# A fourth pair by seven products in the first gate block, two more in the second down block, and three groups of stored sums formed by adding transfers

## The chip, the cores and the metric

One NeuronCore of one Trainium2 chip. The metric is the device time of one execution in microseconds; lower is better. The kernel before was timed in three runs: 1460.48 us in the median (1459.78 to 1462.02).

## The reference, cut to what matters

A block of a hybrid model on 256 rows of 2048 columns, float32 throughout. The change touches the gates and the last product:

```python
proj = h @ w_in                     # h: 256 x 2048; the last 3 * 2048 columns are the gates
...
g = sigmoid(gates.reshape(b, s, 3, 2048) + b_gate)
merged = g[:, :, 0] * (o_fox @ w_br_fox) + g[:, :, 1] * (o_sb @ w_br_sb) + g[:, :, 2] * (o_mem @ w_br_mem)
x = x + merged @ w_out
u = conv(rms_norm(x) @ w_up)        # 2 * 5632 columns
x = x + (silu(u_gate) * u_val) @ w_down     # 256 x 5632 by 5632 x 2048: "down"
```

## The kernel before

**Three passes.** Every large product runs in fp32r: ACT makes a rounded copy `hi` of each weight tile (128 rows by 1024 columns, 512 KB) and DVE the remainder `lo` (`parts`, L349 to L356). Each 128x512 piece of a product is then three matmuls (`three`, L358 to L362): the high part of the activations with `hi`, their low part with `hi`, their high part with `lo`. There are four `hi` and four `lo` buffers.

**Blocks.** A gate, `w_out` or down product is done in blocks of 1024 output columns (`blocked`, L410). A block walks over pairs of 128-row weight tiles (2p and 2p + 1); a *plan*, a string such as `esesesee`, says how each pair is done, in order. `e` (`eight`) is the plain way: two weight tiles, eight 128x512 products, 24 matmuls. `s` is a Strassen-Winograd form with seven products, 21 matmuls. It needs four sums of quarters of the two weight tiles (T1 = B00 + B01, T3 = B01 + B11, T2 = T1 + B11, T4 = T2 + B10) and four sums of the activations' quarters. It has its own four PSUM banks `Y`, which are added into the result (`gathered`) after the block's last seven.

**Where the weights' sums come from.** In the gates `seven_here` is used: DVE forms the four sums from the two loaded tiles (`prepared`, L469 to L476, four additions of 512 columns), one pair ahead. In `w_out` and down `seven` is used (L444): the sums were formed earlier and stored to DRAM, and the pair loads 1.75 MB (two loads of 256 KB, one of 512 KB of the plain weights or sums, then 512 KB and 256 KB of sums) where `e` loads 1 MB. The deque `halves` lists what is to be stored; the helpers `first_sums`, `pair_sums_ahead` and `half_sums` load the plain weights on SP's queue, add on DVE (L252 to L256) and store. 35 pairs are stored, 10 for `w_out` and 25 for down.

**The activations' sums.** For the gates they are formed once for the first `GS = 3` pairs (`x_sums`, in the tile `xs`). For down they are formed by the plan's letter `f` (`form`, then `pair_sums` L365 to L378), 11 in the first down block and 3 in the second. Those of the second block are written over quarters of the activations `aT` that only its first eights still read.

**Order around the change.** The stages follow each other on TensorE: the first gate block done plainly (309.9 to 361.2 us), two gate blocks by plan, the branches, three gate blocks, the branches, `w_out`, up, and from 1232.2 us the two down blocks. In the gates and branches `keep_in_program_order` pins the matmuls; elsewhere the scheduler of the tile framework puts instructions on each engine's queue, and every queue runs in order. SP's queue issues nearly all loads; a load waits until DVE has read the buffer's last tenant (four such buffers in the gates, six in down). POOL's queue is idle between 338 and 760 us; at 760.2 us it moves the row scales of the hidden state.

Of the kernel before, what the change touches and what calls it, by code (L numbers as in the profile page):

```python
# [34 lines left out]
WBUFS = 4  # L35
SBUFS = 4
BLOCKS = 14
GS = 3
PF = (6, 5)
DU = 22  # L40

# [2 lines left out]
def hybrid_block(  # L44
# [159 lines left out]
    def k_tiles(name):  # L204
# [20 lines left out]


    o_plans = ("eessssse", "eessssse")
    g_plans = (("", "esesesee", "esesesee"), ("esesesee", "esesesee", "esesesee"))
    d_plans = (
        "efefefef" + "sef" * 4 + "ssefsfssfssee",  # L230
        "efefef" + "sss" + "esss" * 3 + "ssee",
    )
    T1, T3, T4, T2 = range(4)
    FS2, FS4, FS3, FS1 = range(4)
    in_order = tc.keep_in_program_order
    dram = ctx.enter_context(tc.tile_pool(name="dram", bufs=1, space=bass.MemoryType.DRAM))
    by_k = lambda w: w[0].rearrange("(k p) n -> p k n", p=P)
    o_sevens = (0, 1, 2, 3, 6)
    pairs = lambda name, n: o_sevens if name == "o" else range(n)
    sums_of = {}  # L240
    ordered = [False]
    halves = deque(
        (name, by_k(w), nb, pr, h)
        for name, w, plans in (("o", w_out, o_plans), ("d", w_down, d_plans))
        for nb, plan in enumerate(plans)
        for pr in pairs(name, plan.count("s"))
        for h in range(2)
    )

# [35 lines left out]
    def pair_sums_ahead(staging, period, add, store, most=99, delay=0):  # L285
# [31 lines left out]
        while due:  # L317
            step()
            clock += 1
            yield  # L320

    def first_sums():

# [75 lines left out]
    def blocked(name, w, nb, n0, plan, pair, sums, raw_tile, t4_tile, gathered, ready=None, form=None, apart=None):  # L399
# [1 line left out]
        wv = by_k(w)  # L401
        X = [[bank(f"x{name}{nb}_{t}_{n}") for n in range(2)] for t in range(NT)]
        Y = []
        ns = plan.count("s")

        def a_of(p, j, t):
            v = pair(p, j)
# [34 lines left out]
                                three(apart[0], *a_of(p, j, t), wj, j == 0, j == 1)  # L442

        def seven(p, first, last):  # L444
            kept = sums_of[name, nb, p]
# [6 lines left out]
            raw3 = t4_tile(f"raw_t4_{name}{nb}_{p}")  # L452
# [12 lines left out]
            three(X[1][0], *a_of(p, 1, 1), T4w)  # L465
            go_on()
# [27 lines left out]
        by_seven = seven_here if name == "g" else seven  # L494
        ahead = {}
        s, e = 0, 0
        sp = pairs(name, ns)
        ep = [p for p in range(len(plan) - plan.count("f")) if p not in sp]
        for i, c in enumerate(plan):
            if c == "s":  # L500
                if s == 0:
                    if ready:
                        ready()
                    Y += [bank(f"y{name}{nb}_{j}") for j in range(4)]
                by_seven(sp[s], s == 0, s == ns - 1)
                s += 1
                if s == ns:
                    later(gathered(n0, Y))
# [210 lines left out]
    w = {}  # L719
# [348 lines left out]
    for m in range(2):  # L1068
        gate = []
        for b, plan in enumerate(g_plans[m]):  # L1070
# [52 lines left out]
            for n in range(2):  # L1123
                scaled_sums(n, [X[t][n] for t in range(NT)], [g[n][:, t] for t in range(NT)])
                nc.scalar.activation(g[n], g[n], AF.Sigmoid)
        if m == 1:
            later(merged_sums())
        for n in range(2):
# [190 lines left out]
    def s_of(p, f):  # L1319
# [7 lines left out]
            return sf_more[0][:, f] if f < 2 else sf_rest[2]  # L1327
        if p == 10:
            return sf[:, 27] if f == 0 else sf_rest[f - 1]
        return a_blocks[:, 2 * (p - N0 + N1) + f // 2, :, f % 2]  # L1330

    tmp_d = lambda name: place([P, PIECE], F32, "ts", name)

# [66 lines left out]
```

## Time and profile before

| | |
|---|---|
| median of three runs | 1460.48 us |
| the profiled execution's own time | 1460.56 us |
| its span in the profile | 1458.8 us |
| granted TensorE clock | 1.00 in every slice |
| matmuls by lines L360 to L362 in a run without waits | one every 0.227 us |
| second and third gate block, start to start | 41.5 us, 41.6 us |
| second down block to the end of the span | 112.8 us |
| POOL busy | 21.4 us |

In the rows, PE is TensorE, PEld its weight loads, DVE VectorE, ACT ScalarE, POOL GpSimd and SP the queue that issues loads. A row of a timeline has the start, the duration, the engine, the line and the tiles; in brackets stands idle time before it and what ended it. Matmuls overlap, so that each lasts 0.39 us while the next starts 0.227 us after it. A tile `raw_...` is loaded from DRAM, `hi_...` and `lo_...` are its two parts, `t_...` holds sums, `kept_...` is a pair's sums in DRAM.

### The profile page before, as it was taken

To read this page: it belongs to the slowest core of one execution; us is meant where nothing else is said; L and a number is where in the kernel's file an instruction comes from. 1 tells how busy PE (TensorE), PEld (TensorE's weight loads), DVE (VectorE), ACT (ScalarE), POOL (GpSimd) and SP (SyncE) were. 2 spreads that over 40 slices of the span, in tenths; PEclk is the share of its full clock that TensorE was granted. 3 is DMA by queue.
4 is the path that set the end of the run, shared out by engine and by line. 5 is a ranking of instruction groups with operands and counts; after the bars stand their busy time and mean duration, and the time that the engine had idled before them with its cause. 6 is when DMAs were issued, how large, how long until landed. Compare 5 with 4: busy or idle time off the path is not lost.

```text
span 1458.8 us, 20569 instructions
## 1 busy us (share of the span) xinstructions
PE 1452.1 (100%) x7295; PEld 1228.4 (84%) x7295; DVE 1221.8 (84%) x1804; ACT 851.9 (58%) x1210; POOL 21.4 (1%) x52
## 2 busy tenths in 40 slices
PE   9999999999999999999999999999999999999998
PEld 7888878888888888888888888888888888888887
DVE  5788778776898899998987888888888877999878
ACT  6755445464564555546766656556556565676665
POOL 0000010010000000000000000000000000000000
PEclk9999999999999999999999999999999999999999
DMA  8797899777668576788877888888888866789896
GB/s 290 228 352 247 320 323 333 266 250 217 212 206 268 176 226 201 271 266 261 304 213 231 290 275 299 282 270 299 286 278 298 272 197 201 253 283 341 293 334 220
DMA packets 166502, 387.64 MB, mean 266 GB/s; under 512 B 12554, under 2 KB 29854, under 8 KB 162174
## 3 DMA queue, kind: packets, MB, share of 16 engines
q1 hardware_dynamic: 164702, 383.29, 79.2%
q10 hardware_dynamic: 1328, 2.11, 0.4%
q8 instruction: 57, 0.93, 0.3%
q0 software_dynamic: 368, 0.93, 0.2%
q14 instruction: 47, 0.39, 0.1%
HBM read 347.47 MB, written 38.80 MB: 265 GB/s over the span
## 4 chain that ended last, share of the span: by engine, by line
PE 95%; issue 1%; DVE 1%; DMA 1%; SPq 0%; ACT 0%; POOL 0%; DVEq 0%; POOLq 0%; ACTq 0%
PE u L1289 22%; PE u L1290 11%; PE xg L362 4%; PE xg L361 4%; PE xg L360 4%; PE xd L360 4%; PE xd L362 3%; PE xd L361 3%; PE s L362 2%; PE f L360 2%; PE s L360 2%; PE f L362 2%; PE f L361 2%; PE b L362 2%; PE s L361 2%; PE b L361 2%
## 5 line engine op out<-in xcount | busy, mean ns | idle before, releaser
L1289 PE MATMUL u<-hT,hi_u 128*128 128x512 f32 x1232 | 428.5, 394 | 0.0
L1290 PE MATMUL u<-hT,lo_u 128*128 128x256 f32 x1232 | 341.5, 277 | 0.0
L1289 PEld LDWEIGHTS u<-hT,hi_u 128*128 128x128 f32 x1232 | 231.0, 188 | 53.4
L144 DVE TENSOR_TENSOR lo_u<-raw_u,hi_u 128x1024 fp32r<-128x1024 f32 x176 | 215.5, 1225 | 72.1 <-ACT hi_u L143 71.8
L143 ACT CAST hi_u<-raw_u 128x1024 fp32r<-128x1024 f32 x176 | 184.7, 1050 | 132.7 <-PE u L1289 107.0
L1290 PEld LDWEIGHTS u<-hT,lo_u 128*128 128x128 f32 x1232 | 231.5, 188 | 0.0
L355 DVE TENSOR_TENSOR lo_d<-raw_d,hi_d 128x1024 fp32r<-128x1024 f32 x88 | 106.8, 1223 | 16.7 <-ACT hi_d L354 14.3
L354 ACT CAST hi_d<-raw_d 128x1024 fp32r<-128x1024 f32 x88 | 91.8, 1053 | 39.9 <-PE xd L361 14.3
L354 ACT CAST hi_g<-raw_g 128x1024 fp32r<-128x1024 f32 (+1 forms) x80 | 77.0, 972 | 48.5 <-PE xg L361 19.2
L355 DVE TENSOR_TENSOR lo_g<-raw_g,hi_g 128x1024 fp32r<-128x1024 f32 (+1 forms) x80 | 88.7, 1121 | 4.1 <-ACT hi_g L354 4.1
L362 PE MATMUL xg<-lo_g,xT 128*128 128x512 f32 x175 | 68.1, 389 | 0.0
L360 PE MATMUL xg<-hi_g,xT 128*128 128x512 f32 x175 | 68.1, 389 | 0.0
L361 PE MATMUL xg<-hi_g,xT 128*128 128x512 f32 x175 | 68.1, 389 | 0.0
L143 ACT CAST hi_f<-raw_f 128x1024 fp32r<-128x1024 f32 (+1 forms) x40 | 38.5, 966 | 46.3 <-PE f L361 30.7
L144 DVE TENSOR_TENSOR lo_s<-raw_s,hi_s 128x1024 fp32r<-128x1024 f32 (+1 forms) x40 | 44.5, 1119 | 24.4 <-ACT hi_s L143 24.4
L1289 PE MATMUL u<-hT_rest,hi_u 128*128 128x512 f32 x176 | 62.0, 394 | 0.0
L143 ACT CAST hi_s<-raw_s 128x1024 fp32r<-128x1024 f32 (+1 forms) x40 | 38.4, 962 | 38.2 <-PE s L361 26.5
L143 ACT CAST hi_b<-raw_b 128x1024 fp32r<-128x1024 f32 x32 | 33.7, 1052 | 45.4 <-PE b L361 18.6
L1240 ACT ACTIVATE y<-u,taps 128x256 f32<-128x256 f32 x88 | 49.5, 595 | 17.0 <-DVE u L1235 16.8
L144 DVE TENSOR_TENSOR lo_f<-raw_f,hi_f 128x1024 fp32r<-128x1024 f32 (+1 forms) x40 | 44.4, 1117 | 16.9 <-ACT hi_f L143 16.9
L360 PE MATMUL xd<-hi_d,aT 128*128 128x512 f32 x148 | 57.6, 389 | 0.0
L362 PE MATMUL xd<-lo_d,aT 128*128 128x512 f32 x148 | 57.6, 389 | 0.0
(551 smaller groups left out, 3484.0 us busy)
## 6 DMA issues: line engine op xcount, KB each, us to landing
raw_u<-in_w_up_dram SPq DMA_DIRECT2D x176, 512.0 KB, 4.8
raw_g<-in_w_in_dram SPq DMA_DIRECT2D x96, 512.0 KB, 4.5
raw_d<-in_w_down_dram SPq DMA_DIRECT2D x63, 512.0 KB, 5.6
pre_d<-in_w_down_dram SPq DMA_DIRECT2D x17, 1024.0 KB, 7.2
kept_d<-pre_d SPq DMA_DIRECT2D x17, 1024.0 KB, 6.7
raw_f<-in_w_in_dram SPq DMA_DIRECT2D x32, 512.0 KB, 5.8
raw_s<-in_w_in_dram SPq DMA_DIRECT2D x32, 512.0 KB, 6.1
raw_t_d<-kept_d SPq DMA_DIRECT2D x25, 512.0 KB, 5.8
```

Source lines behind the costliest of these rows:

```text
L143: pin(nc.scalar.copy(hi[:, :m], raw[:, :m]))
L144: pin(nc.vector.tensor_tensor(lo[:, :m], raw[:, :m], hi[:, :m].bitcast(F32), ALU.subtract))
L354: nc.scalar.copy(hi[:, :n], src)
L355: nc.vector.tensor_tensor(lo[:, :n], src, hi[:, :n].bitcast(F32), ALU.subtract)
L360: fix(nc.tensor.matmul(o, lhsT=ah, rhs=w[0], start=first, stop=False))
L361: fix(nc.tensor.matmul(o, lhsT=al, rhs=w[0], start=False, stop=False))
L362: fix(nc.tensor.matmul(o, lhsT=ah, rhs=w[1], start=False, stop=last))
L1240: nc.scalar.activation(y, u[:, 2:], AF.Identity, scale=tap(2), bias=tap(3))
L1289: nc.tensor.matmul(ps[i], lhsT=hi[:, j, c], rhs=hT(k + j), start=first, stop=False)
L1290: nc.tensor.matmul(ps[i][:, :S], lhsT=lo[:, j, c], rhs=hT(k + j)[:, :S], start=False, stop=last)
```

## The change

Three edits that belong together:

- The first gate block by plan goes from `esesesee` to `esesestee`: one `e` fewer, and a letter `t` that is `seven` with stored sums, for pair 3. `GS` goes from 3 to 4, so `x_sums` forms a fourth pair. The stored sums of this pair come first in `halves` (they take the place of the first pair of `w_out` in `first_sums`, and everything behind moves by one).
- The second down block goes from 14 sevens, 8 eights and 3 forms to 16, 6 and 5, in another order.
- The sums of its pairs 13, 14 and 15 leave `halves`, which therefore has 35 pairs as before. A new generator `sums_in_hbm` forms each on POOL's queue: one copy of 1 MB from `w_down` into the stored tile, and four transfers of 256 KB that add. It runs once after each of the gate blocks 01, 02 and 10 (the three that follow each other by plan, counted by half and branch).

```diff
-GS = 3
+GS = 4
...
-    g_plans = (("", "esesesee", "esesesee"), ("esesesee", "esesesee", "esesesee"))
+    g_plans = (("", "esesest" + "e", "esesesee"), ("esesesee", "esesesee", "esesesee"))
     d_plans = (
         "efefefef" + "sef" * 4 + "ssefsfssfssee",
-        "efefef" + "sss" + "esss" * 3 + "ssee",
+        "efsss" * 3 + "efssfsssssee",
     )
+    in_hbm = deque(("d", 1, pr) for pr in range(13, 16))
...
-        for name, w, plans in (("o", w_out, o_plans), ("d", w_down, d_plans))
+        for name, w, plans in (("g", w_in[:, :, C_GATE:], ("", "", "s")), ("o", w_out, o_plans), ("d", w_down, d_plans))
...
+    def sums_in_hbm(behind):
+        name, nb, pr = in_hbm.popleft()
+        mark = cst.tile([P, 1], F32, tag="rows", name=f"mark_{pr}")
+        in_order(nc.gpsimd.tensor_copy(mark, behind))
+        kept = kept_for(name, nb, pr)
+        b = by_k(w_down)[:, 2 * pr : 2 * pr + 2, nb * PIECE : (nb + 1) * PIECE]
+        b = b.rearrange("p k (n c) -> p k n c", n=2)
+        in_order(nc.gpsimd.dma_start(kept.rearrange("p (k n) c -> p k n c", k=2), b))
+        for dst, src in ((0, b[:, 0, 1]), (1, b[:, 1, 1]), (3, kept[:, 0]), (2, kept[:, 3])):
+            in_order(nc.gpsimd.dma_start(kept[:, dst], src, accum_op=ALU.add))
...
-                by_seven(sp[s], s == 0, s == ns - 1)
+                (seven if c == "t" else by_seven)(sp[s], s == 0, s == ns - 1)
...
                 nc.scalar.activation(g[n], g[n], AF.Sigmoid)
+            if in_hbm:
+                sums_in_hbm(g[1][:, 1, 511:])
...
-        return a_blocks[:, 2 * (p - N0 + N1) + f // 2, :, f % 2]
+        i = 3 * (p - N0) + f
+        return a_blocks[:, 2 * N1 + i // 2, :, i % 2]
```

How instructions move on three queues. First DVE, at the end of the first gate block by plan (`lo_g01_12` is the `lo` part of weight tile 12 of that block, `g_0_1_0` the gate that `gathered` writes). Before:

```order
L355 TENSOR_TENSOR lo_t_g01_5_3701<-t1_g01_2_3668,hi_t_g01_5_3700 128x1024
L355 TENSOR_TENSOR lo_g01_12_3713<-raw_g01_12_3710,hi_g01_12_3712 128x1024
L1083 SCALAR_TENSOR_TENSOR g_0_1_0_3729<-yg01_0_3501,scales_111,bg_0_1_3497 128x512
L355 TENSOR_TENSOR lo_g01_13_3737<-raw_g01_13_3734,hi_g01_13_3736 128x1024
L1088 TENSOR_TENSOR gw_0_1_3728<-gw_0_1_3728,yg01_1_3502 128x512
L355 TENSOR_TENSOR lo_g01_14_3759<-raw_g01_14_3756,hi_g01_14_3758 128x1024
```

Now:

```order
L368 TENSOR_TENSOR lo_t_g01_5_3709<-t1_g01_2_3676,hi_t_g01_5_3708 128x1024
L368 TENSOR_TENSOR lo_g01_6_3728<-raw_g01_6_3718,hi_g01_6_3727 128x1024
L368 TENSOR_TENSOR lo_g01_7_3738<-raw_g01_7_3721,hi_g01_7_3737 128x1024
L368 TENSOR_TENSOR lo_t_g01_3_3748<-raw_t_g01_3_3723,hi_t_g01_3_3747 128x1024
L368 TENSOR_TENSOR lo_t4_g01_3_3758<-raw_t4_g01_3_3725,hi_t4_g01_3_3757 128x512
L1096 SCALAR_TENSOR_TENSOR g_0_1_0_3783<-yg01_0_3509,scales_111,bg_0_1_3505 128x512
L368 TENSOR_TENSOR lo_g01_14_3767<-raw_g01_14_3764,hi_g01_14_3766 128x1024
```

Two subtractions of a whole tile have become three and a half, and the gathering starts after them, one eight later than before.

Second POOL, between its last `sb` row and the move of the row scales, where before there was nothing; the first of the three groups (`mark_13` is one column, there to wait for the gate's sigmoid; the waits are on semaphores of ACT and of POOL's own transfers, DMASW):

```order
L327 COPY mark_13_3818<-g_0_1_1_3784 128x1 [waits DMAHW2_49,DMAHW5_49,DMAHW1_49,DMAHW6_49,DMAHW0_49,Activation_49]
L331 DMA kept_d1_13_3820<-in_w_down_dram 256x1x1024
L333 DMA kept_d1_13_3820<-in_w_down_dram 128x512 [waits DMASW4_49]
L333 DMA kept_d1_13_3820<-in_w_down_dram 128x512
L333 DMA kept_d1_13_3820<-kept_d1_13_3820 128x512 [waits DMASW5_49]
L333 DMA kept_d1_13_3820<-kept_d1_13_3820 128x512 [waits DMASW7_49]
```

So a group is four steps one behind the other: the copy, the first two additions together, the third, the fourth.

Third SP's loads at the end of the second down block. Before, in the fourteenth and last seven and behind it:

```order
L416 DMA raw_d1_27_13682<-in_w_down_dram 128x1024
L451 DMA raw_t_d1_13_13684<-kept_d1_13_11046 128x2x512
L453 DMA raw_t4_d1_13_13686<-kept_d1_13_11046 128x512
L416 DMA raw_d1_40_13725<-in_w_down_dram 128x1024
L416 DMA raw_d1_41_13743<-in_w_down_dram 128x1024
```

Now, from the end of the fourteenth seven on:

```order
L466 DMA raw_t4_d1_13_13682<-kept_d1_13_3820 128x512
L460 DMA raw_d1_28_13721<-in_w_down_dram 128x512
L461 DMA raw_d1_28_13721<-kept_d1_14_4179 128x512
L429 DMA raw_d1_29_13724<-in_w_down_dram 128x1024
L464 DMA raw_t_d1_14_13726<-kept_d1_14_4179 128x2x512
L466 DMA raw_t4_d1_14_13728<-kept_d1_14_4179 128x512
L460 DMA raw_d1_30_13767<-in_w_down_dram 128x512
```

The last run of sevens, five before, is seven now (pairs 9 to 15, with the last form between the second and the third of them).

More of the change, by code (lines that the diff above doesn't have):

```diff
@@ L238, in hybrid_block @@
     o_sevens = (0, 1, 2, 3, 6)
-    pairs = lambda name, n: o_sevens if name == "o" else range(n)
+    pairs = lambda name, n: o_sevens if name == "o" else range(GS - n, GS) if name == "g" else range(n)
     sums_of = {}
@@ L243, in hybrid_block @@
         (name, by_k(w), nb, pr, h)
-        for name, w, plans in (("o", w_out, o_plans), ("d", w_down, d_plans))
+        for name, w, plans in (("g", w_in[:, :, C_GATE:], ("", "", "s")), ("o", w_out, o_plans), ("d", w_down, d_plans))
         for nb, plan in enumerate(plans)
         for pr in pairs(name, plan.count("s"))
+        if (name, nb, pr) not in in_hbm
         for h in range(2)
@@ L403, in blocked @@
         Y = []
-        ns = plan.count("s")
+        ns = plan.count("s") + plan.count("t")
         def a_of(p, j, t):
@@ L444, in seven @@
         def seven(p, first, last):
-            kept = sums_of[name, nb, p]
+            kept = sums_of["g", 2, p] if name == "g" else sums_of[name, nb, p]
             raw0 = raw_tile(f"raw_{name}{nb}_{2 * p}")
@@ L451, in seven @@
             nc.sync.dma_start(raw2.rearrange("p (n c) -> p n c", n=2), kept[:, 0:4:3])
-            raw3 = t4_tile(f"raw_t4_{name}{nb}_{p}")
+            raw3 = t4_tile(f"raw_t4_{name}{nb}_{p}")[:, :512]
             nc.sync.dma_start(raw3, kept[:, T4])
@@ L496, in blocked @@
         s, e = 0, 0
-        sp = pairs(name, ns)
+        sp = range(ns) if name == "g" else pairs(name, ns)
         ep = [p for p in range(len(plan) - plan.count("f")) if p not in sp]
         for i, c in enumerate(plan):
-            if c == "s":
+            if c in "st":
                 if s == 0:
```

## The prediction

> **What bounds the kernel now.** I read the page's busy times and its chain of waits first, then TensorE's matmuls one by one, then the windows by stage.
>
> ```profile
> PE 1452.1 (100%) x7295; PEld 1228.4 (84%) x7295; DVE 1221.8 (84%) x1804; ACT 851.9 (58%) x1210; POOL 21.4 (1%) x52
> PE 95%; issue 1%; DVE 1%; DMA 1%; SPq 0%; ACT 0%; POOL 0%; DVEq 0%; POOLq 0%; ACTq 0%
> ```
>
> TensorE is 95% of the chain. A matmul lasts 0.39 us, but they overlap, so I take its cost from starts; this is the timeline of an eight in down:
>
> ```profile
> 1304.27 0.39 PE L360 MATMUL xd<-hi_d,aT 128*128 128x512 f32 x1
> 1304.49 0.39 PE L361 MATMUL xd<-hi_d,aT 128*128 128x512 f32 x1
> ...
> 1309.71 0.39 PE L360 MATMUL yd<-hi_d,aT 128*128 128x512 f32 x1
> ```
>
> 24 matmuls in 5.44 us are 0.227 us each; a seven (21) takes 4.76 us. So the time is matmuls times 0.227 us, as long as DVE and the loads are early enough. Where are they not? The windows by stage (columns: span, busy time of PE, PEld, DVE, ACT, POOL with counts, clock, DMA share, GB/s):
>
> ```profile
> 58.50:193.30 134.80, 134.80 (x674) 114.44 (x673) 104.39 (x175) 70.13 (x121) 2.71 (x4) 1.00 0.85 295
> ...
> 309.90:361.20 51.30, 51.30 (x242) 43.22 (x241) 37.77 (x56) 27.98 (x43) 3.83 (x12) 1.00 0.79 254
> 361.20:402.70 41.50, 41.50 (x185) 34.37 (x184) 36.55 (x44) 24.89 (x27) 0.00 (x0) 1.00 0.64 203
> 402.70:444.30 41.60, 41.60 (x185) 34.31 (x184) 38.14 (x46) 24.32 (x26) 0.00 (x0) 1.00 0.70 225
> ...
> 530.00:572.00 42.00, 42.00 (x186) 34.49 (x185) 38.84 (x48) 23.90 (x25) 0.00 (x0) 1.00 0.68 214
> ...
> 1346.00:1458.80 112.80, 108.85 (x486) 90.21 (x484) 91.05 (x107) 68.26 (x82) 0.00 (x0) 1.00 0.82 284
> ```
>
> In the gate blocks 01, 02 and 11 (from 361, 403 and 530 us) DVE is busy 88 to 92%, while the DMA engines have the most room. DVE's timeline in the block after the changed one, and the matmuls that wait for it there and in the same place of block 11:
>
> ```profile
> 388.15 1.23 DVE L355 TENSOR_TENSOR lo_t_g<-t_g,hi_t_g 128x1024 fp32r<-128x1024 f32 x1 [0.81 <-ACT hi_t_g L354]
> 389.29 1.22 DVE L355 TENSOR_TENSOR lo_g<-raw_g,hi_g 128x1024 fp32r<-128x1024 f32 x1
> 390.43 0.75 DVE L1083 SCALAR_TENSOR_TENSOR g<-yg,scales,bg 128x512 f32<-128x512 f32 x1
> ...
> 398.75 0.69 DVE L472 TENSOR_TENSOR t_g<-raw_g 128x512 f32<-128x512 f32 x1 [0.58 <-DMA raw_g<-in_w_in_dram]
> ...
> 406.86 0.69 DVE L475 TENSOR_TENSOR t_g<-t_g,raw_g 128x512 f32<-128x512 f32 x1
> 407.46 1.23 DVE L355 TENSOR_TENSOR lo_g<-raw_g,hi_g 128x1024 fp32r<-128x1024 f32 x1
> ...
> 414.00 0.69 DVE L473 TENSOR_TENSOR t_g<-raw_g,raw_g 128x512 f32<-128x512 f32 x1 [0.17 <-DMA raw_g<-in_w_in_dram]
> ...
> 420.27 0.69 DVE L472 TENSOR_TENSOR t_g<-raw_g 128x512 f32<-128x512 f32 x1 [1.50 <-DMA raw_g<-in_w_in_dram]
> 420.88 1.22 DVE L355 TENSOR_TENSOR lo_t_g<-t_g,hi_t_g 128x1024 fp32r<-128x1024 f32 x1
> ```
>
> ```profile
> 409.26 0.39 PE L362 MATMUL xg<-lo_g,xT 128*128 128x512 f32 x1
> 422.18 0.47 PE L362 MATMUL xg<-lo_t_g,xT 128*128 128x512 f32 x1
> ```
>
> ```profile
> 550.39 0.39 PE L361 MATMUL xg<-hi_t_g,xT 128*128 128x512 f32 x1
> 550.75 0.50 PE L362 MATMUL xg<-lo_t_g,xT 128*128 128x512 f32 x1
> ```
>
> The `lo_t` that DVE ends at 420.88 + 1.22 = 422.10 is used at 422.18: no cover. In block 11 the same matmul even started 0.36 us after its neighbour instead of 0.227. What leads there is a chain of two loads: DVE ends a `lo` at 407.46 + 1.23 = 408.69, which frees a buffer; the load into it is waited for at 414.00; that lets DVE free the next one, whose load DVE awaits 1.50 us, to 420.27, and the `lo_t` stands behind it in DVE's queue. So **in these blocks each microsecond by which DVE or a load is late at this chain is a microsecond of the kernel**, though TensorE looks busy.
>
> **The change, part by part.** *Matmuls.* Three pairs lose 3 matmuls each (one in the gates, two in down): 9 x 0.227 = **2.04 us** is the most that can be won; forms, sums and loads are not on TensorE.
>
> *The letter t.* It replaces an eight (two whole `lo`) by three whole ones and a half one. DVE's starts give the costs: 390.43 - 389.29 = 1.14 us a whole tile, 407.46 - 406.86 = 0.60 us for 512 columns. That is 1.14 + 0.60 = 1.74 us more on DVE between 389.29 and the `lo` at 407.46. DVE ran there without a hole but one, 0.58 us at 398.75, which the new work fills: 1.74 - 0.58 = 1.16 us later at the head of the chain. The eight that gave DVE room to gather is gone, and loads and `hi` buffers at the block's end come in another rhythm, for which I add 0.2 us (bounds 0 and 0.8, one more wait of the length of that at 388.15): 1.4 us. The `lo` of 407.46 itself has 0.57 us of cover (ready 408.69, used 409.26), but the loads that wait for its buffer have none, so the block's end moves by **+1.4 us** (bounds 1.16 - 0.57 = +0.6, if the loads behind it catch up, and 1.16 + 0.8 = +2.0). The 0.68 us won on matmuls are inside this: TensorE only waits longer. The fourth pair of activation sums lies in the plain gate block, where DVE is busy 37.77 of 51.30 us; I cost it at nothing, and at 2 us if that cover is gone. The stored sums for `t` displace others one for one: nothing.
>
> *The adding transfers.* Their price is not in the trace: no transfer adds, none goes from DRAM to DRAM. The nearest rows are the loads of a stage with a 1 MB load and a 1 MB store beside it (`f`, `s`), against the gates, and POOL's own transfers:
>
> ```profile
> raw_g<-in_w_in_dram SPq DMA_DIRECT2D x96, 512.0 KB, 4.5
> raw_f<-in_w_in_dram SPq DMA_DIRECT2D x32, 512.0 KB, 5.8
> raw_s<-in_w_in_dram SPq DMA_DIRECT2D x32, 512.0 KB, 6.1
> ...
> ck<-ck_row POOLq DMA_DIRECT2D x1, 512.0 KB, 9.4
> ```
>
> A load beside 1 MB transfers takes 5.95 us instead of 4.5: +1.4 us for a load that meets the copy, and half of that, +0.7, for one that meets the two additions of 256 KB. Which meet? The copy waits for the block's second sigmoid:
>
> ```profile
> 405.17 1.06 ACT L1125 ACTIVATE g<-g 128x1024 f32<-128x1024 f32 x1 [0.19 <-DVE g L1108]
> ```
>
> It ended at 406.23 and comes about 2 us later now (the 1.4 us, and a `hi_t` that ACT takes before it). The first load of the chain is asked for at 408.69 + 1.4 = 410.1 us: it meets the copy. By the row of 9.4 us the copy lands near 418, when the second load is asked for (about 418.7), beside the first additions. So block 02 is later by 1.4 + 0.7 = **+2.1 us**. For block 11, behind block 10, the same places:
>
> ```profile
> 541.33 1.06 ACT L354 CAST hi_g<-raw_g 128x1024 fp32r<-128x1024 f32 x1 [0.77 <-PE yg L361]
> ```
>
> ```profile
> 542.26 0.70 DVE L473 TENSOR_TENSOR t_g<-raw_g,raw_g 128x512 f32<-128x512 f32 x1
> ...
> 548.87 0.69 DVE L472 TENSOR_TENSOR t_g<-raw_g 128x512 f32<-128x512 f32 x1 [1.84 <-DMA raw_g<-in_w_in_dram]
> ```
>
> There the first load was in by 541.33, 0.9 us ahead of DVE, so 0.5 of its 1.4 us shows; the second is waited for and adds 0.7: **+1.2 us**. The group behind block 02 lies beside the branches, whose tightest `lo` is this:
>
> ```profile
> 446.65 1.22 DVE L144 TENSOR_TENSOR lo_b<-raw_b,hi_b 128x1024 fp32r<-128x1024 f32 x1
> ```
>
> ```profile
> 450.16 0.39 PE L362 MATMUL b<-lo_b,oT 128*128 128x512 f32 x1
> ```
>
> 2.3 us of cover for 1.4: nothing, and +1 us if it is used up by then. Bounds for the transfers: 0, and 4.9 us (9.4 - 4.5) on one load in each of the two blocks, 9.8 us. I take 3.3 us, near the rows of plain loads, because each group is only 2 MB of data against a DMA share of 0.64 to 0.70. Beside that 9.4 us stands what the Trainium skill's page "DMA: Bandwidth & Descriptors" (Anatomy of one DMA) fits for POOL's path, 2.0 us plus bytes over 436 GB/s: as an estimate 4.4 us for the copy of 1 MB, where the trace shows 9.4 us for half as much; by it the additions would be over before the second loads, and the sum 1.4 us lower.
>
> *The second down block.* Two pairs save 2 x 0.68 = 1.36 us. A seven loads 1.75 MiB = 1.835 MB in 4.76 us, 386 GB/s; the engines give less:
>
> ```profile
> 1374.00:1388.00 14.00, 14.00 (x64) 11.59 (x63) 10.14 (x10) 8.51 (x11) 0.00 (x0) 1.00 0.99 349
> ```
>
> ```profile
> 1437.03 1.05 ACT L354 CAST hi_d<-raw_d 128x1024 fp32r<-128x1024 f32 x1 [0.42 <-DMA raw_d<-in_w_down_dram]
> ```
>
> ```profile
> 1442.39 2.36 DVE L355 TENSOR_TENSOR lo_d<-raw_d,hi_d 128x1024 fp32r<-128x1024 f32 x2
> ```
>
> ```profile
> 1444.19 0.39 PE L362 MATMUL xd<-lo_d,a_ends 128*128 128x512 f32 x1
> ```
>
> At 349 GB/s a seven needs 5.26 us, 0.5 more than it lasts. In the run of five at the end ACT begins to wait for loads (1437.03), and the first `lo` behind it is ready at 1442.39 + 1.22 = 1443.61, 0.58 us before 1444.19. Two more sevens take 2 x 0.5 us: 0.4 us short. Half an eight then refills; I take 0.3 us. DVE has 91 of 112.8 us to do there and gets 2 x 1.74 us and two forms more, which fits into the 22 idle if the forms do not wait; the quarters of `aT` that they write are free halfway through the eight before. Together **-1.1 us** (bounds -1.36 and +2.1, if all seven sevens of the run run at the loads' pace: 7 x 0.5 = 3.5).
>
> *Sum.* +1.4 + 2.1 + 1.2 - 1.1 = +3.6 us on an execution of 1460.56 us, 0.1 us over the median of the runs. I forecast **1464.2 us**, slower by 0.25%.
>
> **The rivals.**
> - *The transfers hide.* If the loads of the two chains land as fast as in the trace, the 3.3 us fall away: +1.4 - 1.1 = +0.3, 1460.8 us, not slower. For it: DMA share 0.64 to 0.70, and each group spread over four steps. Against: two loads in a row have no cover, and the copy starts just before the first. It decides at a delay of 2.6 us for both blocks together, below which the change cannot be told from none.
> - *The group is quick.* If copy and first additions are over when the second loads are asked for, only the first load of each chain is late: 2 x 0.7 us less, 1462.8 us. It decides at some 9 us (409.5 to 418.7) from the copy's issue to the landing of the first additions; the row of 9.4 us for half a copy speaks against it.
> - *The count alone.* DVE finds room for `t` too, and nothing runs out: -2.0, 1458.4 us. Against it is the missing cover at 422.10.
> - *The second down block starves.* The run of seven goes at the loads' pace, 3.5 us in place of 0.3: 1464.2 + 3.2 = 1467.4 us. For it is the share of 0.99; against it, the same `esss` cycles ran without a stall.
> - *POOL's transfers are slow ones.* Each chain is held for 4.9 us: +1.4 + 9.8 - 1.1, 1470.6 us. For it is the 9.4 us row alone.
>
> **How the numbers follow.** Forecast 0.46, hidden transfers 0.24, a quick group 0.08, the count alone 0.06, starved loads 0.10, slow transfers 0.06. About 0.2%, 2.9 us, is what a measurement of this kernel can tell: above 1463.4 is slower, below 1457.6 faster. The forecast's own range is 1462.7 to 1466 us; about a quarter of its chance lies below 1463.4. Slower: 0.34 + 0.10 + 0.06 = 0.50. The same: 0.12 + 0.24 + 0.08 and a third of 0.06, 0.46. Faster: the rest, 0.04, since 2.04 us of matmuls are not 2.9 and something else would have to help. The range 1459 to 1468 takes in the hidden, the quick and the starved case and leaves out the two ends.
>
> **What would show it.** The profile after has 9 matmuls fewer and still 0.227 us a matmul. Step by step: block 02 longer than 41.6 us by 2 to 4 us, with a DVE wait for `raw_g` at L473's and L472's new lines of more than 5.3 us over blocks 01 and 02; block 11 longer than 42.0 us by 1 to 2; median landing of `raw_g` near 5; the second down block shorter by about 1 us with a TensorE wait near its end. I am wrong if both gate blocks keep their length (the transfers hide), if the fourth activation sums delay block 01's start, or if TensorE stalls in down by over 1 us.

## The result and the profile after

The median after is 1467.05 us (1465.58 to 1468.82), against 1460.48 us before: ratio 1.0044, 95% interval 1.0032 to 1.0057. The change makes the kernel 6.6 us slower. The profiled execution took 1466.73 us with a span of 1465.0 us, so 6.2 us more of span than before have to be explained from its trace.

From the page of the kernel after, busy times, chain and landing of the gate loads:

```profile
PE 1454.1 (99%) x7286; PEld 1228.5 (84%) x7286; DVE 1233.0 (84%) x1831; ACT 859.7 (59%) x1225; POOL 61.4 (4%) x70
PE 92%; DVE 4%; DMA 2%; issue 2%; POOL 0%; ACT 0%; DVEq 0%; ACTq 0%; POOLq 0%
raw_g<-in_w_in_dram SPq DMA_DIRECT2D x95, 512.0 KB, 4.6
```

There are nine matmuls fewer, as the change says, and yet the span is longer: the chain that was TensorE's at 95% now leads through DVE and DMA at 6%. The median landing of `raw_g` moved by 0.1 us only, so it says nothing of where the loss is. The windows from block to block do. Of before (branches, block 10, 11, 12, second down block; blocks 01 and 02, 41.48 and 41.57 us, stand in the prediction with rounded borders), then of after, with blocks 01 and 02:

```profile
444.26:488.75 44.49, 44.49 (x202) 36.84 (x200) 38.37 (x51) 19.41 (x21) 0.00 (x0) 1.00 0.76 243
488.75:531.12 42.37, 42.37 (x192) 35.19 (x191) 36.75 (x44) 22.77 (x26) 0.00 (x0) 1.00 0.61 194
531.12:572.87 41.75, 41.75 (x185) 34.28 (x183) 38.59 (x47) 23.90 (x26) 0.00 (x0) 1.00 0.68 214
572.87:614.38 41.51, 41.51 (x185) 34.35 (x184) 39.19 (x48) 24.32 (x26) 0.00 (x0) 1.00 0.70 226
...
1344.60:1458.80 114.20, 110.25 (x492) 91.35 (x491) 92.45 (x109) 68.26 (x82) 0.00 (x0) 1.00 0.82 282
```

```profile
361.26:402.06 40.80, 40.80 (x181) 33.79 (x180) 36.27 (x42) 26.71 (x29) 0.00 (x0) 1.00 0.68 219
402.06:445.50 43.44, 42.09 (x185) 34.21 (x183) 37.13 (x45) 23.11 (x24) 15.04 (x6) 1.00 0.83 252
445.50:491.54 46.04, 44.82 (x202) 36.75 (x200) 36.81 (x48) 20.49 (x22) 8.79 (x7) 1.00 0.93 276
491.54:537.88 46.34, 44.33 (x192) 36.27 (x191) 41.62 (x51) 23.07 (x26) 0.00 (x0) 0.96 0.65 198
537.88:579.58 41.70, 41.70 (x184) 34.27 (x183) 37.11 (x44) 23.89 (x26) 16.10 (x6) 1.00 0.86 255
579.58:622.46 42.88, 42.10 (x184) 34.13 (x183) 40.78 (x51) 24.31 (x26) 0.00 (x0) 1.00 0.73 223
...
1352.36:1465.00 112.64, 108.85 (x486) 90.20 (x484) 99.39 (x129) 73.51 (x94) 0.00 (x0) 1.00 0.85 303
```

Block 01 is 0.7 us shorter, its three matmuls. Block 02 is 1.9 us longer, the branches 1.55, block 10 4.0, block 11 nothing, block 12 1.4; the second down block is 1.6 us shorter. Together that is 6.5 us, against 6.2 us of span; the 0.3 us between them lie in small differences elsewhere.

Which engine holds TensorE there? These are its waits between 361 and 1260 us in the kernel after (total, times, longest); in the kernel before this answer has no row at all:

```profile
PE mt L1053 <- DVE g L1157: 2.0, 1, 2.0
PE xg L375 <- DVE lo_g L368: 1.5, 2, 0.8
PE b L375 <- DVE lo_b L144: 1.2, 1, 1.2
PE yg L375 <- DVE lo_g L368: 0.6, 1, 0.6
```

The `yg` and the first `xg` wait stand at 408.71 and 410.45 us, the start of block 02; the wait at `b` at 452.77, the start of the branches; that of the `mt` transposes at 499.37, in block 10; the second `xg` at 587.28, the start of block 12. What is late is seen on POOL's timeline:

```profile
408.97 11.29 POOL L327 COPY mark<-g 128x1 f32<-128x1 f32 x1 [69.42 <-ACT g L1138]
420.20 0.67 POOL L331 DMA_DIRECT2D kept_d<-in_w_down_dram  x1
427.75 1.76 POOL L333 DMA_DIRECT2D kept_d<-in_w_down_dram  x2 [6.87 <-DMA kept_d<-in_w_down_dram]
437.48 0.81 POOL L333 DMA_DIRECT2D kept_d<-kept_d  x1 [7.97 <-DMA kept_d<-in_w_down_dram]
444.94 0.81 POOL L333 DMA_DIRECT2D kept_d<-kept_d  x1 [6.64 <-DMA kept_d<-kept_d]
452.81 4.63 POOL L327 COPY mark<-g 128x1 f32<-128x1 f32 x1 [7.06 <-ACT g L1138]
457.38 0.70 POOL L331 DMA_DIRECT2D kept_d<-in_w_down_dram  x1
```

The mark, a copy of one column, took 11.29 us. The first group's copy was issued at 420.20 us, when the loads of block 02's chain were through, and the group's last addition only at 444.94 us, just ahead of the branches; the second group then lay on the branches, from 457.38 us to its last addition, issued at 484.69. The landing of `raw_b`, the branches' loads, went up (least, median, most of all 32 of them, which takes in the branches' second turn; before, then after):

```profile
DMA to landing us min/median/max: 4.4/5.7/6.2
```

```profile
DMA to landing us min/median/max: 3.7/7.6/9.3
```

ACT waits for those loads (22.0 us from 444 to 501 us, where it waited 1.8 before), DVE for ACT, and at the end of the branches DVE's queue is so late that the last gate products, which the transposes need, come 2 us after TensorE asks.

### The profile page after: what moved, and what is told of

Read it like the earlier page. It is cut to its first block, busy times and chain, and to the rows that moved or that the text cites. A ratio compares the mean times of both kernels' runs of the same rounds, so it can differ in the third digit from the quotient of the medians.

```text
span 1465.0 us, 20657 instructions
## 1 busy us (share of the span) xinstructions
PE 1454.1 (99%) x7286; PEld 1228.5 (84%) x7286; DVE 1233.0 (84%) x1831; ACT 859.7 (59%) x1225; POOL 61.4 (4%) x70
## 3 DMA queue, kind: packets, MB, share of 16 engines
q10 hardware_dynamic: 1328, 2.11, 0.4%
## 4 chain that ended last, share of the span: by engine, by line
PE 92%; DVE 4%; DMA 2%; issue 2%; POOL 0%; ACT 0%; DVEq 0%; ACTq 0%; POOLq 0%
PE u L1304 22%; PE u L1305 11%; PE xd L375 3%; PE xd L374 3%; PE xd L373 3%; PE xg L375 3%; PE xg L373 3%; PE xg L374 3%; PE s L375 2%; PE f L375 2%; PE s L373 2%; PE f L373 2%; PE f L374 2%; PE s L374 2%; PE yd L375 2%
## 5 line engine op out<-in xcount | busy, mean ns | idle before, releaser
L373 PE MATMUL xg<-hi_g,xT 128*128 128x512 f32 x168 | 65.7, 391 | 0.0
L374 PE MATMUL xg<-hi_g,xT 128*128 128x512 f32 x168 | 65.6, 391 | 0.0
L367 ACT CAST hi_t_d<-raw_t_d 128x1024 fp32r<-128x1024 f32 (+1 forms) x54 | 43.5, 835 | 18.5 <-PE xd L374 11.6
L373 PE MATMUL s<-hi_s,xT 128*128 128x512 f32 (+1 forms) x140 | 53.7, 384 | 0.0
```

The costliest lines, as they stand in the source:

```text
L367: nc.scalar.copy(hi[:, :n], src)
L373: fix(nc.tensor.matmul(o, lhsT=ah, rhs=w[0], start=first, stop=False))
L374: fix(nc.tensor.matmul(o, lhsT=al, rhs=w[0], start=False, stop=False))
```

## Experiments

Twelve kernels were run. All times are differences of medians from the kernel before on the same chip. The ratio takes in every run, so that it can lie a little off these differences where single runs are long; its interval stands behind it.

**The parts alone.** First the fourth pair without the groups:

```diff
-    in_hbm = deque(("d", 1, pr) for pr in range(13, 16))
+    in_hbm = deque()
...
-        "efsss" * 3 + "efssfsssssee",
+        "efefef" + "sss" + "esss" * 3 + "ssee",
```

> The fourth pair t and its stored sums alone: no adding transfers, the second down block with its 14 sevens as before. Theory A (the trace of after: t makes TensorE wait 0.75 + 0.93 us at the start of block 02, and everything lost later comes from the transfers): three matmuls fewer, -0.7, and 1.7 of waits, so 1.0 us above before; no wait of TensorE over 0.3 us in the branches or in block 10. Rival B (the waits in the branches and in block 10 are an echo of t, whose 1.7 us of VectorE work is never caught up): 5 to 7 us above before, with the waits at lo_b and between the transposes of mt in the trace as in after.

Measured: +1.55 us, ratio 1.0015 (1.0006 to 1.0025). TensorE waits only at the start of block 02 (0.8 + 0.94 us between starts), and nowhere later. Theory A stands, the echo of rival B does not exist. VectorE's `lo` at the head of block 02, which started at 407.46 us before, now comes 1.72 us later:

```profile
409.18 1.21 DVE L368 TENSOR_TENSOR lo_g<-raw_g,hi_g 128x1024 fp32r<-128x1024 f32 x1
```

Behind the chain's second load nothing of it is left: the `lo_t` there starts at 420.75 us, before at 420.88.

Then the groups without the fourth pair:

```diff
-GS = 4
+GS = 3
...
-    g_plans = (("", "esesest" + "e", "esesesee"), ("esesesee", "esesesee", "esesesee"))
+    g_plans = (("", "esesesee", "esesesee"), ("esesesee", "esesesee", "esesesee"))
...
-        for name, w, plans in (("g", w_in[:, :, C_GATE:], ("", "", "s")), ("o", w_out, o_plans), ("d", w_down, d_plans))
+        for name, w, plans in (("o", w_out, o_plans), ("d", w_down, d_plans))
```

> The three groups of adding transfers behind blocks 01, 02 and 10 and the second down block with 16 sevens, without the fourth pair: the first gate block has its three sevens as before. Theory A: -1.4 from six matmuls fewer, and the waits of after from the branches on, 1.4 + 2.3 + 1.6 (matmuls at twice their period behind the wait of 2.3) + 0.9 = 6.2, so 4.8 us above before. Rival B: the transfers stay hidden without t, and the time is 1 us below before. Theory C, the recorded prediction's: block 02 longer by 2.1, block 11 by 1.2, second down block 1.1 shorter, so 2.2 us above before.

Measured: +5.0 us, ratio 1.0035 (1.0023 to 1.0047). The size is that of theory A, the place is not: it is block 02, which theory C names at half the price. Here DVE let the mark through after 7.57 us, the copy was issued at 413.36 us, and it met the chain of block 02:

```profile
422.31 0.69 DVE L485 TENSOR_TENSOR t_g<-raw_g 128x512 f32<-128x512 f32 x1 [4.00 <-DMA raw_g<-in_w_in_dram]
```

```profile
424.19 0.50 PE L375 MATMUL xg<-lo_t_g,xT 128*128 128x512 f32 x1 [2.11 <-DVE lo_t_g L368]
```

DVE waited 1.50 us for this load before the change, now 4.00, and TensorE stands; the additions were issued at 422.40 us, too late to have a part in it. Block 02 took 45.53 us instead of 41.57, while the branches lost nothing, block 10 0.4 us and block 12 0.7. So here the first group costs 4 us, and which stage pays depends on when the mark gets through. The second group lay on the branches as in the kernel after (from 456.87 us, its last addition issued at 483.84) and yet cost 0.4 us at most. TensorE had come to the branches 3.7 us later than before, and this delay, paid already, may well have covered it; then the prices of groups that follow each other do not add up. No run separates that. The six runs lay between 1463.37 and 1469.44 us and the profiled one is the fastest of them, so its trace shows less than the median lost.

**Is it the mark?** The mark is written by ACT and then by a memset, so that GpSimd reads no SBUF:

```diff
-        in_order(nc.gpsimd.tensor_copy(mark, behind))
+        in_order(nc.scalar.copy(mark, behind))
+        in_order(nc.gpsimd.memset(mark, 0.0))
```

> All of the change, but the mark that holds each group back is written by ACT (one column) and then by a GpSimd memset, so that GpSimd reads no SBUF for it. Theory A (GpSimd's copy of one column took 4.6 to 12.2 us because VectorE kept it from reading; the transfers then start that much later): the memset takes under 1 us, the first copy is issued at 409 to 410 us instead of 420, and its wait falls on loads of block 02, as in the kernel with the groups alone (2.3 us and some 1.4 us of slow matmuls), while the waits in the branches, 1.4 and 2.3, shrink; in all within 2 us of after, 4 to 9 us above before. Rival E (the late start is what costs): the time falls to 2 us above before or less.

Measured: +13.2 us, ratio 1.0088 (1.0071 to 1.0104). POOL, then DVE in block 11:

```profile
411.19 0.10 POOL L328 MEMSET mark<- 128x1 f32 x1 [69.96 <-ACT mark L327]
411.23 0.68 POOL L332 DMA_DIRECT2D kept_d<-in_w_down_dram  x1
...
545.03 0.71 POOL L332 DMA_DIRECT2D kept_d<-in_w_down_dram  x1
```

```profile
553.81 0.69 DVE L487 TENSOR_TENSOR t_g<-raw_g,raw_g 128x512 f32<-128x512 f32 x1 [2.52 <-DMA raw_g<-in_w_in_dram]
...
563.02 0.69 DVE L486 TENSOR_TENSOR t_g<-raw_g 128x512 f32<-128x512 f32 x1 [4.45 <-DMA raw_g<-in_w_in_dram]
```

The mark takes 0.10 us, so it was GpSimd's reading that was held up. But the late start was a shelter: with the copy on time, both loads of block 11's chain are waited for, and that block took 49.69 us against 41.75 before. Rival E falls. Theory A has the memset and, nearly, the copy's start, but neither the size (9 us at most) nor the places: block 02 took 44.80 us, only 1.4 us more than in the kernel after, the branches 47.41 us, which is longer than there and not shorter, and most of the loss lies in block 11, which theory A does not name. The profiled execution is the slowest of the four.

**The second group out of the branches.** Groups 1 and 3 stay; the sums of the second are formed in eight steps of 256 KB in the up stage (`steps_of`, shown further down), one behind every 18th piece:

```diff
-            if in_hbm:
+            if (m, b) in ((0, 1), (1, 0)):
                 sums_in_hbm(g[1][:, 1, 511:])
...
+    whole = deque([("d", 1, 13), ("d", 1, 15)])
+    small = steps_of("d", 1, 14)
```

> All of the change, with the first and third group as they are (behind blocks 01 and 10) and the second, which ran beside the branches, in 8 small steps in the up stage. Theory A (the second group's late raw_b made VectorE late for the transposes of mt: 2.3 us of wait and 1.6 us of slow matmuls): those 3.9 us go, 2.7 us above before; the waits at the start of block 02, at lo_b (1.4) and before block 12 (0.9) stay. Rival K (the lateness comes from the first group's tail): within 1 us of after.

Measured: +2.0 us, ratio 1.0017 (1.0009 to 1.0026), 4.6 us less than after. Its window of block 10:

```profile
491.83:534.20 42.37, 42.37 (x192) 35.19 (x191) 37.17 (x45) 22.78 (x26) 0.00 (x0) 1.00 0.64 197
```

That is 42.37 us as before the change: the wait of the transposes and the slow matmuls are gone. The wait at `lo_b`, right behind the first group's last addition, stayed (2.0 us). So in the kernel after the second group costs those 4 us, and block 10 pays them; it does so behind the letter t and the first group's tail: without t, and with the first group's last addition issued 9.7 us before the branches (438.30 us, groups alone), the same group cost 0.4 us.

**Another place.** The groups are moved to the up stage, with and without the fourth pair:

```diff
-            if in_hbm:
-                sums_in_hbm(g[1][:, 1, 511:])
...
+                if (s, k) == (1, 0) and f0 in (8, 16, 24):
+                    sums_in_hbm(hi[:, 0, 511:].bitcast(F32))
                 tick()
```

> All of the change, but the three groups of adding transfers are issued in the up stage (behind a piece of its 5th, 9th and 13th half-rounds, some 90 us apart), not behind gate blocks. Theory A (the price is that of the place: branches and gate blocks have loads that cannot come later): +1.0 for t, -1.4 in down, the up stage as long as before within 0.5, so 0.4 us below before. Rival D (7 MB of software-queue transfers cost what they cost anywhere, since raw loads land later beside them): the 6 us move to the up stage, 5 to 7 us above before.

> The groups of adding transfers in the up stage as in the kernel before this one, and no fourth pair in the first gate block: only the second down block's two additional sevens are left of the change. Theory A: six matmuls fewer and no new wait, 1.4 us below before, ratio 0.999. Rival D: 4 to 6 us above before.

Measured: +9.9 us (ratio 1.0060, 1.0048 to 1.0072) and +8.1 us (1.0057, 1.0045 to 1.0069). Theory A fell here, and rival D named less than was measured. The up stage, before and in the second of these kernels:

```profile
742.20:1232.16 489.96, 489.96 (x2833) 428.86 (x2832) 408.77 (x668) 292.39 (x451) 1.29 (x2) 1.00 0.81 264
```

```profile
742.42:1244.58 502.16, 497.75 (x2833) 431.91 (x2832) 404.55 (x665) 291.15 (x451) 15.00 (x20) 1.00 0.83 266
```

It is 12.2 us longer, though TensorE never waited in it before and DVE has more room than in the gates. The profiled execution is the slowest of its five, and not all of the 12.2 us are waits. Set against the kernel before matmul by matmul, 6.8 us are lost within 30 us of a group's start; the other 5.4 us come slowly, above all from 880 to 959 us and from 1064 us to the end of the stage, with no wait of TensorE and a granted clock of 1.00. In 30 us without and with this slower pace (from 1000 us, as in the kernel before, and from 1100 us):

```profile
1000.00:1030.00 30.00, 30.00 (x175) 26.45 (x174) 26.62 (x47) 18.56 (x29) 0.00 (x0) 1.00 0.89 321
1100.00:1130.00 30.00, 30.00 (x172) 26.03 (x171) 26.19 (x42) 17.30 (x24) 0.00 (x0) 1.00 0.83 277
```

The slower pace sets in behind a wait; what brings it on and what ends it stays open. The 6.8 us are the loads'. From 855 to 885 us of that kernel (queues with their share of 16 engines, then loads with their median landing), beside the same stretch of the kernel with copies only, below:

```profile
q0 software_dynamic: 596, 1.12, 26.3%
raw_u<-in_w_up_dram SPq DMA_DIRECT2D x9, 512.0 KB, 11.5
```

```profile
q0 software_dynamic: 23, 0.08, 0.7%
raw_u<-in_w_up_dram SPq DMA_DIRECT2D x10, 512.0 KB, 9.1
```

In the kernel before a load of this stage lands in 4.8 us. At 11.5 us it no longer fits: TensorE takes a piece every 490 / 176 = 2.78 us, and four buffers cover, as an estimate, 11.1 us. With copies only the longest landing from 840 to 885 us was 10.9 us and TensorE did not wait; with whole groups it was 13.2 us.

**Bytes, bursts or additions?** One kernel forms the same sums in 24 steps of 256 KB, spread over the stage; another leaves the additions out (its last three sevens use plain columns):

```diff
+        for i in (0, 1, 3, 2):
+            yield to(i, b[:, i // 2, i % 2])
+            src = (b[:, 0, 1], b[:, 1, 1], kept[:, 3], kept[:, 0])[i]
+            yield to(i, src, accum_op=ALU.add)
```

```diff
-        for dst, src in ((0, b[:, 0, 1]), (1, b[:, 1, 1]), (3, kept[:, 0]), (2, kept[:, 3])):
-            in_order(nc.gpsimd.dma_start(kept[:, dst], src, accum_op=ALU.add))
```

> No fourth pair; the same sums of three groups formed in the up stage, but in 24 steps of 256 KB (a copy and an adding transfer for each of the four tiles of a pair), each behind its own mark, six pieces (some 17 us) apart. Theory F (a burst costs: the whole group in 30 us doubled the landing of raw_u to 9.8 us and ran the four buffers out, though a fifth of the DMA time in this stage is free): no wait of TensorE over 0.5 us in up, 1.4 us below before. Rival D (bytes and additions cost the same wherever and however they are spread): 8 us above before, as with three groups.

> As the kernel with the groups in the up stage and no fourth pair (8.1 us above before), with the four adding transfers of each group left out: the second down block's last three sevens use plain columns instead of sums. Theory G (the price is memory traffic: 2 of a group's 5 MB are the copy's): 0.4 of 9.5 us is left, 2 to 3 us above before. Rival H (it is the 1 MB copy that floods the queues, the adding transfers of 256 KB are cheap): 7 to 9 us above before. Rival I (it is the additions): within 1 us of 1.4 us below before.

Measured: -0.9 us (ratio 1.0000, 0.9988 to 1.0013) and -1.4 us (0.9989, 0.9980 to 0.9999). Both are as fast as the six matmuls allow, within what the runs can tell: 9 us of price vanish either way. In the spread kernel up takes 490.00 us, at a DMA share of 0.85 instead of 0.81, and `raw_u` lands in 5.9 us. The reading that fits both is that it is neither bytes nor additions by themselves but what stands on the DMA engines within one pipeline's depth (the 11.1 us above), and that in this sum the additions weigh double; where the limit lies was not measured. From section 3 of the pages (packets, MB, share), with three whole groups in up and with their copies alone:

```profile
q0 software_dynamic: 2912, 7.22, 2.3%
```

```profile
q0 software_dynamic: 1184, 4.07, 0.9%
```

Before it was 0.93 MB and 0.2%. The copies' 3.14 MB took 0.7% of the engines' time and the additions' 3.15 MB 1.4%: an adding transfer holds the engines about twice as long for a byte. Its packets are half as large (1728 for these bytes, the copies' 816), so that it need not be the adding itself.

The same cut at the gates:

> As the kernel with the groups alone behind blocks 01, 02 and 10 (5.0 us above before), with the four adding transfers of each group left out: the second down block's last three sevens use plain columns instead of sums. Theory I (the additions are what costs, here too): no wait over 0.5 us in block 02, 1.4 us below before, or 1.0 us at most above that. Rival J, the recorded prediction's split (1.4 of block 02's 2.1 us are the 1 MB copy's, which meets raw_g): the copy alone costs 2.3 us and slow matmuls behind it, 2 to 3 us above before.

Measured: -1.35 us, ratio 0.9994 (0.9985 to 1.0002), and no wait in block 02. But here DVE held the mark for 12.25 us and the copy was issued at 419.24 us, behind the chain's loads, so this run cannot say what a copy costs that meets them; the kernel with the groups alone can, above. Further on it does say something: the branches took 44.49 us, block 10 42.37 and block 12 41.48, as before the change, though a copy was issued beside the branches at 453.33 us. Without the additions those stages pay nothing; with them, in the profile of the groups alone, block 10 paid 0.4 us and block 12 0.7.

All of the change, with the small steps in up:

> All of the change with the fourth pair, but the three groups' sums formed in 24 small steps in the up stage. Theory: the sum of the two parts run alone, +1.5 (fourth pair alone) and -0.9 (small steps without it), so 0.6 us above before; waits of 1.7 us at the start of block 02, none over 0.5 us in the branches, block 10 and up. Rival B (the stored sums of t and those of the groups crowd each other): 3 us above before or more.

Measured: -0.2 us, ratio 0.9999 (0.9991 to 1.0008). The two parts add up within their intervals; nothing crowds.

**Small steps in the gates.** If spreading and free DMA time are what counts, the gate blocks with 30 to 39% of it should do better than up. The steps stand behind their pieces:

```diff
+        def go_on():
+            if name == "g":
+                small_step(last[-1][:, 511:].bitcast(F32), 4, 3)
+            tick(beside=name != "g")
```

> No fourth pair; the three groups' sums in 24 steps of 256 KB within the five gate blocks by seven, one behind every third piece (some 8 us apart), each held back by a mark that ACT and a GpSimd memset write. Theory F (what counts is DMA time that is free beside the step; here 30 to 37% is free against 19% in up): no wait of TensorE over 0.5 us, 1.4 us below before. Rival L (a gate block by seven has loads without slack at its chains, t_g waited 1.50 us for raw_g in before, so that every step that meets one costs, free time or not): 3 to 8 us above before.

Measured: +14.8 us, ratio 1.0097 (1.0085 to 1.0109), the clearest miss of theory F, and more than rival L's 3 to 8 us. DVE's waits from 360 to 625 us, and TensorE's:

```profile
DVE t_g L505 <- DMA raw_g<-in_w_in_dram: 22.2, 9, 5.6
...
PE xg L385 <- DVE lo_t_g L378: 7.7, 5, 3.0
```

(The profiled execution is the fastest of the five.) The share of free time is the wrong measure there. A gate block by seven asks for two loads in a row that nothing covers; a step that meets one of them costs, and 24 steps meet them often.

**Without GpSimd.** Last, the same two sevens more, with all sums formed by VectorE in up, a pair every 7 pieces instead of 8:

```diff
-        pair_sums_ahead(lambda name: ends_tile(name, F32).rearrange("p i c -> p (i c)"), 8, 1, 5, delay=DU)
+        pair_sums_ahead(lambda name: ends_tile(name, F32).rearrange("p i c -> p (i c)"), 7, 1, 5, delay=DU)
```

> No fourth pair and no transfer on GpSimd's queue: the sums of pairs 13 to 15 of the second down block are formed like the others, by VectorE from a 1 MB load that SP issues in the up stage and stores again, for which one such pair is taken up every 7 pieces instead of every 8 (19 pairs in the stage instead of 17). Theory (the price of the change is the adding transfers, not the two sevens more, and the up stage has room for two more pairs on VectorE, busy 409 of 490 us there, and on the DMA engines, busy 0.81): 1.4 us below before, ratio 0.999, as with the copies only; no wait of TensorE over 0.5 us in up. Rival M (7 pieces, 19.5 us, are too short for a load, the sums and a store through one buffer, so that SP waits and raw_u comes late): 2 us above before or more.

Measured: +18.2 us, ratio 1.0118 (1.0101 to 1.0135); up took 512.61 us (in the slowest of the four runs) at a *lower* DMA share, 0.78. SP's waits from 740 to 1260 us, those for the store of the sums, which in the kernel before have 5.6 us in all:

```profile
SPq L297 <- DVE y L1261: 19.5, 4, 6.2
SPq L297 <- DVE aT L178: 15.4, 3, 7.4
...
SPq L297 <- DVE pre_d L256: 13.5, 10, 3.8
```

SP stands at the store until DVE has come to the sums, and the loads of `raw_u` stand behind it. Rival M is right, through the queue's order and not through bytes.

No version is shown to beat both kernels. The small steps in up without the fourth pair come nearest (1459.65 us), and beat only the one after.

## Why the prediction was right or wrong

1. *Direction and size.* 1464.2 us was forecast, slower by 3.7 us; measured were 1467.05 us and 6.6, inside the range. That the total came out in the range is in part luck: the largest term was paid at twice its size and mostly in other stages (5). The chance of slower was 0.50, no more, because the price of the transfers was taken low.
2. *Matmuls.* Nine fewer at 0.227 us: right.
3. *The letter t, +1.4 us at the end of block 02.* Right: with it alone that end stands at 445.49 us instead of 444.26, +1.2 us, and the kernel is 1.55 us slower. The place was not the chain of two loads but its head: the first two `lo` of block 02, for which TensorE waits 0.63 and 0.77 us. VectorE was late by 1.72 us there, nearly the whole 1.74, since the hole of 0.58 us did not swallow its part; the cover of 0.57 us was used up; and the loads behind did catch up, which the sum had only as its lower bound. Two errors of the same size cancel, so the closeness of 1.2 to 1.4 is luck.
4. *Fourth activation sums and stored sums, nothing.* Right: block 01 starts at 361.26 us, before at 361.21.
5. *The adding transfers, 2.1 + 0 + 1.2 = 3.3 us.* Mis-sized and in part misplaced; this step failed. In the trace after they cost 1.55 in the branches, 4.0 in block 10 and 1.4 in block 12, 6.9 us. Three things were wrong in it. The copy was to be issued near 409.5 us, right behind the sigmoid; the mark, which was taken for a mere wait, held it until 420.20. So block 02, the term of +2.1, lost nothing beyond t's share, and block 11's +1.2 was not paid either. The mechanism proposed for them is real, as the kernel with the marks free of reads shows, but there block 11 pays 7.9 us and not 1.2. The branches were written off because 2.3 us of cover exceed one load's 1.4 us of delay; but a group lasts some 30 us there and delays some ten loads one behind another, so that the delays add up on ACT and DVE until the cover is gone. That this costs 4 us holds for the kernel after; with the groups alone it cost 0.4.
6. *What the price was drawn from.* The landing of loads beside other 1 MB transfers (+1.4 us) was the wrong row. Beside the copy, in the kernel with the groups alone, DVE waited 4.00 us for the chain's second load instead of 1.50, +2.5 for one load. From their issue to that of the additions behind them the three copies of the kernel after took 7.5, 10.7 and 8.0 us, and the first group's additions were not through before 437.48 us, 17 us after its copy was issued, so the rival of a quick group falls. The Trainium skill's fit ("DMA: Bandwidth & Descriptors", Anatomy of one DMA), by which 1 MB would take an estimated 4.4 us, does not agree with these times.
7. *A cost that was not in the sum.* After the wait of 2 us eight matmuls ran at twice their period, 1.6 us (below). It stands once in the trace after, once in that of the groups alone and, behind a longer wait, in that of the marks free of reads.
8. *Second down block, -1.1 us.* It is 1.56 us shorter between the same places, and TensorE waits nowhere in down; the 0.3 us for the run of seven sevens were not needed. The rival of starved loads, which gave the time that was then measured (1467.4), was right in the number alone.
9. *The signs named in advance.* DVE's waits for `raw_g` in blocks 01 and 02 were to exceed 5.3 us; they fell to 2.8, since DVE itself had become the later one. The landing of `raw_g` was to go to 5; it went to 4.6. Block 02 longer by 2 to 4 us was narrowly missed (1.9), block 11 kept its length. These signs would have said early that the copy came late.

What stays open: in several kernels, with groups and without, single executions lie 5 to 8 us above the fastest (the fourth pair alone: 1461.21 to 1469.45 us), while the kernel before keeps within 4. In the kernels where only one or two runs are that long (the fourth pair alone, both with small steps in up) no profile fell on one of them. The slower pace of TensorE that the profile of the groups in up shows, 5.4 us in one execution, would be of that size; that it is the cause is not shown.

## What to carry to other kernels

Here background transfers were not paid by their share of DMA time but, as far as these kernels show, by how much of it fell within one pipeline's depth of loads that someone waited for: against the six matmuls won, the same transfers cost 9 us in three bursts and next to nothing in 24 steps in a stage with four buffers of slack, and some 6 us in three bursts but 16 us in 24 steps in a stage whose loads have none. Before a stage is called covered, add up the delay of all the loads that lie beside the transfer, not of one. And what starts a background transfer is itself an instruction on an engine's queue: look up what that engine needs. Here a mark that was held up for 11 us moved the price to other stages, and freeing it doubled the loss, from 6.6 to 13.2 us.

## What the runs showed of the hardware

*GpSimd and VectorE.* In the kernel after, GpSimd's copy of one column ended at 420.26 us. VectorE's timeline around it:

```profile
408.57 0.69 DVE L488 TENSOR_TENSOR t_g<-t_g,raw_g 128x512 f32<-128x512 f32 x1
...
419.00 1.22 DVE L368 TENSOR_TENSOR lo_t_g<-t_g,hi_t_g 128x1024 fp32r<-128x1024 f32 x1
420.76 1.23 DVE L368 TENSOR_TENSOR lo_t_g<-t_g,hi_t_g 128x1024 fp32r<-128x1024 f32 x1 [0.55 <-ACT hi_t_g L367]
```

VectorE had run two-operand additions and subtractions back to back since before 409 us; at its first hole, from 420.22 us, the copy came through. With the groups alone the copy ended at 413.42 us, at a hole from 413.37. The second mark of the kernel after ended at 457.44 us without a hole, as VectorE began a multiplication that reads one of its operands from PSUM. The memset in its place took 0.10 us. The Trainium skill's page "SBUF — State Buffer" (SBUF: two separate sides) says that a VectorE operation with two SBUF inputs and a GpSimd operation that reads SBUF lock each other out for an instruction. The runs agree with the lock, and show more: the loser waited through some 12 instructions, not one.

*TensorE's period after a wait.* Behind the wait of 2.01 us that ended at 499.37 us in the kernel after:

```profile
501.24 0.63 PE L373 MATMUL xg<-hi_g,xT 128*128 128x512 f32 x1
501.66 0.63 PE L374 MATMUL xg<-hi_g,xT 128*128 128x512 f32 x1
...
503.80 0.43 PE L373 MATMUL yg<-hi_t_g,xs 128*128 128x512 f32 x1
504.07 0.39 PE L374 MATMUL yg<-hi_t_g,xs 128*128 128x512 f32 x1
```

A matmul starts every 0.43 us instead of 0.227 for 3 us, and the granted clock from 500.80 to 503.80 us is 0.50. The same followed a wait of 2.11 us with the groups alone and one of 4.38 us with the marks free of reads, but not one of 1.98 us (second group in small steps) nor one of 3.01 us (small steps at the gates). So the length of the wait does not decide alone. The page "TensorE: Matmul & The Clock Gate" of the Trainium skill (What's actually happening) has the clock drop after an idle window of about 3.4 us, in windows that run freely. Free-running windows would fit that equal waits differ; the length does not agree, since waits of 2.01 and 2.11 us were enough here.
